# The 512 KB weight loads of the attention stage, moved from SyncE's DMA queue to GpSimd's

## The chip, the cores and the metric

One core of a Trainium2 chip runs the whole kernel. The metric is the device time of one execution in microseconds (us), lower being better.

## What is computed

The kernel is a two-layer decoder trunk for one sequence of 1024 tokens of width 1024. Layer 0 mixes tokens by causal pooling, layer 1 by attention with forget gates ("FoX", 16 heads of 64). Both also attend to 256 memory tokens, gate each branch with SiLU, project and normalise. The part that matters here is layer 1:

```
h = x @ w_in                      # queries u_main, memory queries, gates g_main, g_mem
k, v, cum = shared_kv(x, ...)     # keys, values, cumulative log forget gates
logits[t, s] = q_t . k_s / 8 + cum[t] - cum[s]     # causal, 16 heads
y_main = softmax(logits) @ v
y = concat(y_main * silu(g_main), y_mem * silu(g_mem)) @ w_out
x = layer_norm(alpha * x + y)
```

All inputs are float32 and the result must be close to float32, so each matrix operand is split into a high and a low half, and a product is made of three products of halves.

## The kernel before, in words

**Slabs.** Every projection is cut into slabs: 128 output columns for all 1024 tokens. `slab` (L324) loads the 1024 x 128 weights of one slab as two pieces of 128 x 512 float32, splits each piece into halves, and issues 48 matmuls of 128 x 512. It is a generator: it yields after each matmul, so that a caller can spread its matmuls between other work.

**Two manners of loading.** Early in the kernel each piece has its own 256 KB load on SyncE's queue (`split_w`, L212), and ScalarE and VectorE make the split. In the attention stage the flag `low[0]` is set. Then one load brings both pieces (512 KB, "wide") into a tile of pool B, which has 10 buffers; `slab` yields once, GpSimd splits the first piece, `slab` yields, GpSimd splits the second, `slab` yields, and the matmuls follow. A split on GpSimd (`gp_scaled_hi_lo`, L176 to L178) is three instructions: scale in place (L176), round to float16 (through `gp_copy`, L193), subtract (L178). The halves go into pool w, which has 6 buffers, one for a piece, so that it holds the weights of three slabs. There are 27 wide loads, numbered here from 0 in the order of their splits: gate slab 0; queries and gate of pair 1; then keys, queries and values of pairs 2 to 7, with the gates 2, 4, 7, 3, 5 and 6 between them.

**The attention stage.** `fox` walks through 16 heads and, in each, through 8 tiles of 128 queries, the longest first. A tile makes its logits on TensorE (L323), adds bias and mask and finds the bound of the exponent on VectorE (L1028), takes the exponential on ScalarE (L1036), normalises and splits into halves (L1064, L1065), transposes by DMA on SyncE's queue (L1081) and, six tiles later, multiplies with the values (L1090). The mask of a tile is made by GpSimd (`mask`, L1002), three tiles ahead, in one of the four buffers of pool raw.

**The fill.** TensorE's order is written by hand. Between the steps of a tile, `Fill.pump` issues matmuls of pending slabs, some 10 for a tile. It holds a list of units; the first is the slab at work, the second the next one. As soon as a unit is second in the list its wide load is asked for; when the slab at work has 30 of its 48 matmuls left, the next one's first piece is split, and with 16 left its second piece. The slabs of keys are asked for in other places: their load at the third tile of a pair's second head, their splits at the sixth and seventh. `ask` does the same by hand for gate slab 0, ahead of the stage.

**Queues.** TensorE's instructions stand in the written order. For the other engines a planner orders the instructions by its own simulation, ahead of the run. `tc.keep_in_program_order` pins an instruction behind the one that was written last for the same engine. The masks, the splits and the products with the gates (L1117, L1130) of GpSimd are pinned; the loads on SyncE's queue are not, so the planner may put a wide load as early as a buffer of pool B comes free. An instruction at the head of a queue that waits holds up all behind it. SyncE's queue also carries the transposes (L1081), the moves of keys and queries between partitions (L909), the forget rows (L1009) and all other loads and stores. GpSimd's queue carries 80 loads of weights early in the kernel (`look_ahead`, L258, until 260 us), and none later.

Of the kernel before, what the change touches and what calls it, by code (L numbers as in the profile page):

```python
# [78 lines left out]
def trunk_kernel(ctx, tc, x, xT, memT, win, wk, wv0, wv, wmk, wmv, wout, poolw, pscale, lng, lnb, bforget, out):  # L79
# [5 lines left out]
    nc = tc.nc  # L85
# [21 lines left out]
    def ps(shape, tag, bufs):  # L107
        return psum.tile(shape, F32, tag=tag, name=nm(tag), bufs=bufs)
# [80 lines left out]
    def three(a, b):  # L189
        return (a.hi, b.hi), (a.top, b.lo), (a.lo, b.hi if isinstance(a, Wide) else b.top)  # L190
# [18 lines left out]
    def split_w(src_dram, shape, sc=None, r=None, pin=lambda ins: ins):  # L209
        if r is None:  # L210
            r = raw(shape)
            nc.sync.dma_start(r, src_dram)  # L212
        if sc is not None:
            to = half_of(wt, shape)
            if low[0]:
                gp_scaled_hi_lo(to, r, sc)
            else:
                scaled_hi_lo(to, r, sc, pin)
            return to
        to = parts_of(wt, shape)  # L220
        (gp_hi_lo if low[0] else hi_lo)(to, r)
        return to
# [19 lines left out]
    def look_ahead(see=True):  # L242

        while to_see and len(landed) < 5:
            k, src = to_see.pop(0)
            if not room or src.shape[1] == 2:
                room[:] = [seeing[0]([P, 2 * NH])]
            r = room[0] if len(room) == 1 else room[1]
            if src.shape[1] == 2:
                r = r[:, : 2 * FW].rearrange("p (a b) -> p a b", a=2)  # L250
                room[:] = []
            elif len(room) == 1:
                room.append(r[:, NH:])
                r = r[:, :NH].rearrange("p (a b) -> p a b", a=4)
            else:
                r = r.rearrange("p (a b) -> p a b", a=4)
                room[:] = []
            tc.keep_in_program_order(nc.gpsimd.dma_start(r, src))  # L258
            landed.append((k, r))
        if landed and see:  # L260
            k, r = landed.pop(0)
            if k < 12:
                tc.keep_in_program_order(nc.vector.tensor_reduce(
                    sums[:, k : k + 1], r, AX.XY, ALU.add, apply_absolute_value=True,
                ))
            else:
                tc.keep_in_program_order(nc.scalar.activation(r, r, AF.Abs, accum_out=sums[:, k : k + 1]))
# [57 lines left out]
    def slab(pieces_dram, X, evac, banks=("pj", 2), g=0):  # L325

        arrived = isinstance(pieces_dram, list)
        sc = sws[g] if isinstance(X, Half) else None
        both = (None, None)
        if low[0]:  # L330
            wide = roomy[0]([P, 2, 4, P])
            nc.sync.dma_start(wide, pieces_dram.rearrange("c p k m -> p c k m"))
            both = wide[:, 0], wide[:, 1]
            yield 0
        ws = list(pieces_dram) if arrived else [split_w(pieces_dram[0], [P, 4, P], sc, both[0])]
        if low[0]:
            yield 0
            ws.append(split_w(pieces_dram[1], [P, 4, P], sc, both[1]))
            yield 0
        accs = {}  # L340
        high, low_top = (0,), (1, 2)
        if sc is not None:
            order = [(n, pc, (0, 1, 2)) for n in range(2) for pc in range(2)]
        elif arrived:
            order = [(n, pc, part) for pc in range(2) for n, part in ((0, high), (1, high), (1, low_top), (0, low_top))]
        else:
            order = [(0, pc, part) for part in (high, low_top) for pc in range(2)]
            order += [(1, pc, part) for part in (low_top, high) for pc in range(2)]
        seen = {0: 0, 1: 0}
        for n, pc, part in order:  # L350
            if len(ws) <= pc:
                ws.append(split_w(pieces_dram[pc], [P, 4, P], sc, both[pc]))
            if n not in accs:
                accs[n] = ps([P, NH], *banks)
            for i in part:
                a, b = three(ws[pc], X)[i]
                for k in range(4):
                    seen[n] += 1
                    nc.tensor.matmul(  # L359
                        accs[n], a[:, k, :], b[:, pc * 4 + k, n * NH : (n + 1) * NH],  # L360
                        start=seen[n] == 1, stop=seen[n] == 3 * KT,
                    )
                    if seeing[0]:
                        seeing[1] += 1
                        if seeing[1] % 8 == 0:
                            look_ahead()
                    if seen[n] == 3 * KT:
                        evac(slice(n * NH, (n + 1) * NH), accs[n])
                    yield NH
# [79 lines left out]
    def gate_units(w_dram, dst, X, g=0):  # L449
        half = hun1s[g] if isinstance(X, Half) else 0.5  # L450
        return slab(w_dram, X, lambda cols, acc: gate(acc, dst[:, cols], half), g=g)
# [9 lines left out]
    def mem_attention(l, X, kv, qtile, ytile, yd, behind=None, before=None, last=None):  # L461
# [6 lines left out]
        for h in range(MH):  # L468
            q = parts_of(qtile, [P, S])
            run(slab(win[l, 8 + h], X, lambda cols, acc: q_split(l, q[:, cols], acc)))  # L470
            qs.append(q)
            if not l:
                keys(h)
            vals(h)
# [223 lines left out]
    with tc.tile_pool(name="in0", bufs=1) as in0:  # L698
# [34 lines left out]
        def pool_group(g, see=None):  # L733
            w = WINDOWS[g]
            pms = []
            for f in (2 * g, 2 * g + 1):
                u = sb([P, S], "P", 4)
                run(slab(
                    first[f] if g == 0 else win[0, f], X, lambda cols, acc: nc.scalar.copy(u[:, cols], acc),
                    ("L", 3) if f == 1 else ("pj", 2),  # L740
                ))
                cur, sh = u, 1
                while sh < w:
                    nxt = G()
                    nc.vector.tensor_tensor(nxt[:, sh:], cur[:, sh:], cur[:, : S - sh], ALU.add)
                    nc.vector.tensor_copy(nxt[:, :sh], cur[:, :sh])
                    cur, sh = nxt, 2 * sh
                pm = G()
                nc.vector.scalar_tensor_tensor(pm[:, w - 1 :], cur[:, w - 1 :], 1.0 / w, u[:, w - 1 :], ALU.mult, ALU.subtract)
                nc.vector.tensor_tensor(pm[:, : w - 1], cur[:, : w - 1], invc[:, : w - 1], ALU.mult)  # L750
                nc.vector.tensor_tensor(pm[:, : w - 1], pm[:, : w - 1], u[:, : w - 1], ALU.subtract)
                pms.append(parts_of(T, [P, S]))
                hi_lo(pms[-1], pm)
# [543 lines left out]
```

## Time and profile before

| what | value |
|---|---|
| runs shown | 1189.03, 1192.14 and 1192.09 us; median 1192.09 us |
| the profiled execution | 1191.01 us, of which the span from first to last instruction is 1189.3 us |
| TensorE busy | 1164.2 us, 98% of the span |
| VectorE, ScalarE, GpSimd busy | 781.7, 684.7 and 285.5 us |
| granted TensorE clock | 0.995 |
| DMA | 203.89 MB, 171 GB/s on average |

The stages by time from the span's start: layer 0 until about 455 us, the memory attention of layer 1 to 577 us, first keys, values and forget gates to 645 us, the attention stage to about 1046 us, and then the output projection and the norm. In rows of instructions the columns are the start and the duration in us, the engine, the line and the operation, output<-input and count; in brackets stands how long the engine was idle just before, and who ended it. A row for a line gives minimum, median and maximum duration in ns and the first and last start. In rows of waits the columns are the total in us, how often, and the longest. PE is TensorE, DVE VectorE, ACT ScalarE, POOL GpSimd, SP SyncE; a q behind the name means its queue of instructions.

### The profile page before, as it was taken

What the parts mean: (1) busy time and instruction counts of PE and PEld (TensorE: products, weight loads), DVE (VectorE), ACT (ScalarE), POOL (GpSimd) and SP (SyncE); (2) the same over time, 40 slices, a digit from 0 to 9 for tenths busy, and PEclk for the clock granted to TensorE, in tenths of its full rate; (3) what the DMA queues carried; (4) which work ended last, traced back from release to release, by engine and by line L of the source; (5) the groups of instructions that cost most, each with busy time, mean ns of one, the idle gap of its engine ahead of it and who ended that gap; (6) DMA issues with size and microseconds to landing.
All of it is one profiled execution on the core that took longest, in us unless ns stands there. A gap on an engine that the chain in (4) does not pass through costs nothing. (4 is left out here: it accounts for less than half of the span.)

```text
span 1189.3 us, 19794 instructions
## 1 busy us (share of the span) xinstructions
PE 1164.2 (98%) x6894; PEld 672.1 (57%) x6941; DVE 781.7 (66%) x1840; ACT 684.7 (58%) x1512; POOL 285.5 (24%) x437
## 2 busy tenths in 40 slices
PE   8999999999999999999999999999999999999996
PEld 5566776555555557556674555555555545455553
DVE  6744675555765566447655888778777787874654
ACT  6478875976563234557431776666766677774210
POOL 3321001310000000000002454555554445750000
PEclk8999999999999999999999999999999999999998
DMA  7576656754286544446644789989997999875530
GB/s 259 170 250 193 171 104 213 246 179 148 89 284 170 148 136 121 133 128 124 176 148 113 172 184 220 191 171 204 187 210 150 169 195 204 217 191 171 175 109 35
DMA packets 286196, 203.89 MB, mean 171 GB/s; under 512 B 224912, under 2 KB 238352, under 8 KB 286096
## 3 DMA queue, kind: packets, MB, share of 16 engines
q1 hardware_dynamic: 279696, 181.59, 60.4%
q0 software_dynamic: 6400, 21.04, 5.4%
q8 instruction: 54, 0.88, 0.3%
q14 instruction: 46, 0.38, 0.1%
HBM read 116.01 MB, written 22.61 MB: 117 GB/s over the span
## 5 line engine op out<-in xcount | busy, mean ns | idle before, releaser
L359 PE MATMUL pj<-A,w 128*128 128x512 f16 (+2 forms) x2875 | 662.3, 383 | 4.2 <-DMA A<-A 1.2
L359 PEld LDWEIGHTS <-w 128*128 128x128 f16 (+1 forms) x2560 | 245.7, 98 | 281.2 <-issue 11.3
L1036 ACT ACTIVATE T<-MK,s 128x512 f32<-128x512 f32 x192 | 111.2, 579 | 64.6 <-DVE s L1028 47.7
L1065 DVE SCALAR_TENSOR_TENSOR P<-T,s,P 128x512 f16<-128x512 f32 x192 | 112.0, 613 | 39.1 <-ACT P L1064 38.0
L1064 ACT ACTIVATE P<-T,s 128x512 f16<-128x512 f32 x192 | 103.0, 575 | 53.1 <-issue 28.9
L599 PEld LDWEIGHTS <-T 128*128 128x128 bf16 x736 | 70.6, 98 | 89.8 <-issue 4.4
L1002 POOL TENSOR_SCALAR_AFFINE_SELECT raw<-R 128x256 f32<-128x256 f32 (+3 forms) x128 | 59.4, 466 | 178.7 <-DVE s L1028 96.2
L199 DVE TENSOR_TENSOR w<-raw,w 128x512 bf16<-128x512 f32 x74 | 52.3, 708 | 54.1 <-ACT w L198 36.7
L323 PE MATMUL L<-A 128*128 128x512 f16 (+3 forms) x384 | 84.4, 326 | 3.2 <-DVE s L1028 3.1
L885 POOL MEMSET G<- 128x128 f32 x1 | 0.2, 204 | 335.5 <-DVE V L541 335.5
L359 PEld LDWEIGHTS pj<-A,w 128*128 128x128 f32 x352 | 65.1, 188 | 16.5 <-ACT w L198 1.2
L199 DVE TENSOR_TENSOR T<-T,T 128x1024 bf16<-128x1024 f32 x23 | 28.0, 1219 | 68.8 <-PE pj L599 38.3
L178 POOL TENSOR_TENSOR w<-B,w 128x512 f16<-128x512 f32 x54 | 62.8, 1165 | 4.0
L323 PEld LDWEIGHTS <-A 128*128 128x128 f16 x384 | 37.4, 98 | 46.3 <-issue 4.8
L198 ACT CAST T<-T 128x1024 fp32r<-128x1024 f32 x23 | 24.1, 1047 | 62.6 <-DMA T<-y1d 34.9
L198 ACT CAST w<-raw 128x512 fp32r<-128x512 f32 x76 | 46.7, 615 | 23.2 <-DMA raw<-in_win_dram 9.8
L1090 PEld LDWEIGHTS <-V 128*64 128x64 f16 (+1 forms) x1152 | 50.6, 104 | 12.9 <-issue 5.6
L1090 PE MATMUL O<-T,V 128*64 128x128 f16 (+1 forms) x1152 | 57.5, 220 | 0.0
L599 PE MATMUL pj<-B,T 128*128 128x512 bf16 (+1 forms) x187 | 52.1, 385 | 0.3
L1028 DVE CUSTOM_DVE_ANT_0 MK<-L,R,scales 128x512 f32<-128x512 f32 x64 | 45.3, 708 | 9.8 <-PE L L323 9.4
L200 ACT CAST w<-raw 128x512 bf16<-128x512 f32 x78 | 48.2, 618 | 3.3 <-PE pj L359 1.9
L599 PE MATMUL L<-B,T 128*128 128x512 bf16 (+1 forms) x165 | 47.0, 394 | 0.7 <-ACT T L200 0.5
(289 smaller groups left out, 1843.5 us busy)
## 6 DMA issues: line engine op xcount, KB each, us to landing
raw<-in_win_dram SPq DMA_DIRECT2D x66, 256.0 KB, 3.3
W<-in_win_dram POOLq DMA_DIRECT2D x48, 256.0 KB, 3.8
R<-cumd SPq DMA_DIRECT2D x16, 512.0 KB, 4.4
B<-in_win_dram SPq DMA_DIRECT2D x15, 512.0 KB, 5.0
y0d<-Y SPq DMA_DIRECT2D x12, 512.0 KB, 4.0
raw<-in_wout_dram SPq DMA_DIRECT2D x24, 256.0 KB, 2.7
T<-y0d SPq DMA_DIRECT2D x12, 512.0 KB, 4.5
A<-A SPq DMA_DIRECT2D x24, 256.0 KB, 4.1
```

Source lines behind the costliest of these rows:

```text
L178: pin(nc.gpsimd.tensor_tensor(to.lo, src, to.hi, ALU.subtract))
L198: pin(nc.scalar.copy(to.hi, src))
L199: pin(nc.vector.tensor_tensor(to.lo, src, to.hi.bitcast(F32), ALU.subtract))
L200: pin((top or nc.scalar.copy)(to.top, src))
L323: nc.tensor.matmul(acc, a, b, start=i == 0, stop=i == len(terms) - 1)
L359: nc.tensor.matmul(accs[n], a[:, k, :], b[:, pc * 4 + k, n * NH : (n + 1) * NH], start=seen[n] == 1, stop=seen[n] == 3 * KT,)
L599: nc.tensor.matmul(accs[a][nh], y, w, start=kt == 8 and i == 0, stop=kt == 7 and i == 2,)
L1002: tc.keep_in_program_order(nc.gpsimd.affine_select(C[:, :w], R[:, lo:up], [[-1, w]], ALU.is_ge, -NEG, base=w - P, channel_multiplier=1,))
L1036: nc.scalar.activation(e, p[:, lo:up], AF.Exp, bias=top, scale=-1.0, accum_out=sums[:, n, hd % 2, i : i + 1],)
L1064: nc.scalar.activation(pair[:, lo:up], e, AF.Copy, scale=r)
L1065: nc.vector.scalar_tensor_tensor(pair[:, L + lo : L + up], e, r, pair[:, lo:up], ALU.mult, ALU.subtract)
L1090: nc.tensor.matmul(acc[rows, (i % 4) * P : (i % 4) * P + P], v[:, b, 2 * j : 2 * j + (1 if e else 2), :].rearrange("p e d -> p (e d)"), pt ...
```

## The change

In `slab`, the wide load goes from SyncE's queue to GpSimd's, and it is pinned there behind the GpSimd instruction that was written last. Its source, its destination, its place in the written program and everything else stay.

```diff
         if low[0]:
             wide = roomy[0]([P, 2, 4, P])
-            nc.sync.dma_start(wide, pieces_dram.rearrange("c p k m -> p c k m"))
+            tc.keep_in_program_order(nc.gpsimd.dma_start(wide, pieces_dram.rearrange("c p k m -> p c k m")))
             both = wide[:, 0], wide[:, 1]
             yield 0
```

## The prediction

> **What bounds the kernel now.** I read the page first, then the stretch in which the moved loads work, then TensorE's waits there.
>
> ```profile
> span 1189.3 us, 19794 instructions
> PE 1164.2 (98%) x6894; PEld 672.1 (57%) x6941; DVE 781.7 (66%) x1840; ACT 684.7 (58%) x1512; POOL 285.5 (24%) x437
> PEclk8999999999999999999999999999999999999998
> ```
> ```profile
> 650.00:1050.00 400.00, 395.88 (x2762) 208.67 (x2760) 316.52 (x924) 280.40 (x670) 211.21 (x318) 1.00 0.91 191
> ```
> ```profile
> PE L L323 <- DVE s L1028: 3.1, 6, 1.1
> PE pj L848 <- DVE G L857: 0.7, 1, 0.7
> PE pj L359 <- POOL w L178: 0.7, 1, 0.7
> PE pj L359 <- POOL w L193: 0.2, 1, 0.2
> ```
>
> TensorE is the bound, at full clock. From 650 to 1050 us, where 26 of the 27 wide slabs are multiplied, it is busy 395.88 of 400 us: **all its idle time there is 4.1 us**, 0.35% of the time. The waits (560 to 1060 us) say whose it is: 3.1 us belong to VectorE's softmax, 0.9 us to GpSimd's splits. The gain is capped before anything is worked out; GpSimd at 211.21 of 400 us and DMA at 0.91 are full enough to ask what can be lost.
>
> **What leaves SyncE's queue.** The line of the wide load, and the longest wait it held:
>
> ```profile
> L332 SPq DMA_DIRECT2D B<-in_win_dram x15: 367/720/1467, 517.4 to 1012.9; - x15
> L332 SPq DMA_DIRECT2D B<-in_wk_dram x6: 379/392/674, 580.5 to 792.3; - x6
> L332 SPq DMA_DIRECT2D B<-in_wv_dram x6: 421/678/1069, 581.6 to 824.8; - x6
> DMA to landing us min/median/max: 3.7/5.0/8.6
> ```
> ```profile
> SPq L332 <- POOL w L178: 26.0, 1, 26.0
> ```
>
> 27 issues leave SyncE, by medians 15 x 0.72 + 6 x 0.39 + 6 x 0.68 = 17.2 us, and a 26.0 us block near 601 us. I price both at nothing: TensorE's list of waits holds no transpose, move or forget row; six tiles between transpose and values cover them. If that cover were gone, a late transpose would show as a wait of L1090 on a DMA; there is none.
>
> **What stays in the sum: load 25.** Its row on SyncE comes after two transposes, and GpSimd and TensorE wait for it:
>
> ```profile
> 1007.68 4.38 SPq L1081 DMA_TRANSPOSE T<-P  x2
> 1012.12 1.90 SPq L332 DMA_DIRECT2D B<-in_win_dram  x2
> ```
> ```profile
> 1017.49 1.72 POOL L176 TENSOR_SCALAR B<-B,scales 128x512 f32<-128x512 f32 x2 [4.08 <-DMA B<-in_win_dram]
> ```
> ```profile
> 1018.60 1.03 PE L323 MATMUL L<-A 128*128 128x512 f16 x4
> 1019.85 1.90 PE L359 MATMUL pj<-A,w 128*128 128x512 f16 x8 [0.22 <-POOL w L193]
> 1022.45 1.47 PE L359 MATMUL pj<-A,w 128*128 128x512 f16 x6 [0.71 <-POOL w L178]
> ```
>
> Matmuls start 0.216 us apart (row of 814.72 below: 10 in 2.16 us). So after 1018.60 the next group could start at 1018.60 + 4 x 0.216 = 1019.46 and starts at 1019.85: 0.39 us. After 1019.85 the next could start eight matmuls later, at 1021.58, and starts at 1022.45: 0.87 us. Together **1.26 us**. On GpSimd the load is written where the slab before it begins, 48 matmuls (10.4 us) and some 3 us of logits and values ahead of 1019.85, so near 1006 us; issued by 1008 and 5.0 us under way it lands near 1013 instead of 1017.4. Its two splits then finish near 1018.5, ahead of TensorE. I take the whole 1.26 us off. From both sides: 0, if a buffer of pool B comes free no sooner; 4.1 us, the whole idle time, above.
>
> **What arrives on GpSimd.** The nearest rows are its early loads, half the size, and the splits:
>
> ```profile
> L258 POOL DMA_DIRECT2D W<-in_win_dram x48: 546/546/736, 24.9 to 231.5; - x48
> ```
> ```profile
> DMA to landing us min/median/max: 2.7/3.7/6.9
> ```
> ```profile
> L176 POOL TENSOR_SCALAR B<-B,scales 128x512 f32<-128x512 f32 x54 | 38.3, 709 | 4.6 <-DMA B<-in_win_dram 4.1 <-PE T L323 0.5
> L193 POOL TENSOR_SCALAR w<-B 128x512 f16<-128x512 f32 x54 | 33.7, 625 | 29.9 <-PE pj L359 25.8
> L178 POOL TENSOR_TENSOR w<-B,w 128x512 f16<-128x512 f32 x54 | 62.8, 1165 | 4.0
> ```
>
> A wide issue isn't in the trace for this queue. It describes twice the rows, so I bound it by 0.55 us (no growth) and 1.47 us (twice the slowest), and take twice the median, 1.1 us: 27 x 1.1 = 30 us more on GpSimd, 15 to 40 us by the bounds. What hides it is GpSimd's own waiting for a mask buffer:
>
> ```profile
> POOL raw L1002 <- DVE s L1028: 96.2, 48, 4.4
> POOL raw L1002 <- DVE s L1049: 53.6, 26, 4.7
> ```
>
> It waits 150 us for VectorE to give back a mask buffer, and a mask is made three tiles, some 9 us, before its use. So issues cost nothing on TensorE's path. Without that cover each would delay the logits behind it by its 1.1 us, 30 us at most.
>
> **The new wait.** Until now a wide load lay in SBUF long before its split. Load 12, the thirteenth of both lists, with TensorE's matmuls around it:
>
> ```profile
> 671.18 1.07 SPq L332 DMA_DIRECT2D B<-in_wv_dram  x1
> ```
> ```profile
> 815.83 0.69 POOL L176 TENSOR_SCALAR B<-B,scales 128x512 f32<-128x512 f32 x1
> 816.61 0.62 POOL L193 TENSOR_SCALAR w<-B 128x512 f16<-128x512 f32 x1
> 817.31 1.16 POOL L178 TENSOR_TENSOR w<-B,w 128x512 f16<-128x512 f32 x1
> 818.80 0.69 POOL L176 TENSOR_SCALAR B<-B,scales 128x512 f32<-128x512 f32 x1
> ```
> ```profile
> 812.23 2.54 PE L359 MATMUL pj<-A,w 128*128 128x512 f16 x11
> 814.72 2.32 PE L359 MATMUL pj<-A,w 128*128 128x512 f16 x10
> 816.88 1.03 PE L323 MATMUL L<-A 128*128 128x512 f16 x4
> 817.74 2.54 PE L359 MATMUL pj<-A,w 128*128 128x512 f16 x11
> 823.27 0.38 PE L359 MATMUL pj<-A,w 128*128 128x512 f16 x1
> 824.14 2.32 PE L359 MATMUL pj<-A,w 128*128 128x512 f16 x10
> 827.45 2.54 PE L359 MATMUL pj<-A,w 128*128 128x512 f16 x11
> ```
>
> It was issued 145 us ahead. Counting 48 matmuls from 812.23 (11, 10, 11, 1, 10 and 5), the slab before runs from 812.2 to 828.4, when load 12's first piece is needed. Under the change the load is issued at the start of that slab, about 812.5 to 813.6. Landing by SyncE's median of 5.0 us comes near 818, where the split was at 815.83: **GpSimd waits some 2 us per load**, with the next masks behind it, and TensorE doesn't, since the first split takes 2.64 us (815.83 to 817.31 + 1.16) and has until 828.4. The shortest slab is 48 x 0.216 = 10.4 us plus the logits of at least three tiles, 0.86 us each where long: 13 us. So TensorE is untouched while issue, landing and split fit in 13 us: 13 - 2.6 - 1.1 = **9.3 us for the landing**, against a longest of 8.6 on SyncE and 6.9 on GpSimd. Load 0 is free: its split waited for a weight buffer, not for data.
>
> ```profile
> 623.17 0.62 POOL L193 TENSOR_SCALAR w<-B 128x512 f16<-128x512 f32 x1 [25.83 <-PE pj L359]
> ```
>
> [...]
>
> **The sum.** 1191.01 (the profiled execution; the span is 1.7 us less) - 1.26 = **1189.8 us**. The median of the runs shown is 1.08 us higher than the profiled one; on its footing the sum is 1190.8. The planner will order SyncE, ScalarE and VectorE somewhat differently, which may move the 3.1 us of softmax waits either way; I count nothing for it.
>
> **The rivals.** How full SyncE's queue keeps the 16 DMA engines from 640 to 1050 us:
>
> ```profile
> q1 hardware_dynamic: 175769, 77.40, 89.2%
> ```
>
> - *Late landing; slower.* With 89.2% of their time taken by SyncE's queue, a load in a second queue may be served turn by turn among small packets. From 9.3 us of landing on, TensorE waits; each further us costs 1 us at each of the 19 slabs that the fill asks for (27 less six of keys, gate 0 and gate 7, whose loads are asked three tiles ahead). At 11 us that is 1.7 x 19 = 32 us: 1223. Against it: 8.6 us was the worst on SyncE, behind the transposes of its own queue. Chance 0.09.
> - *Thin places; slower.* GpSimd's 2 us waits delay splits and masks, and where it also stands behind a product with a gate (L1117, which waits for VectorE), nothing is left. With 2 us lost at 3 of the 27 slabs: 1191.0 + 6 - 1.3 = 1195.8 us, up to 1199 with five. The wait on a DMA at L176 in the row of 1017.49 shows that the kind exists. Chance 0.20.
> - *Load 25 no sooner; no change.* Its buffer, not SyncE's queue, held it: 1191.0. Chance 0.12.
> - *The softmax waits go too; faster.* The emptier SyncE queue or new order removes all 4.1 us: 1186.9. Chance 0.06.
>
> **How the numbers follow.** Forecast 0.53; a measurement of this kernel can tell about 0.3%, 3.6 us, from no change. Within it lie the forecast and the third rival, 0.65; faster by more, the fourth, 0.06; slower by more, the first two, 0.29. The range goes from 1186.9, the whole idle time, to 1199, the upper end of thin places, and leaves out the late landing.
>
> **What would show it.** Right: L332 as POOL rows of about 1.1 us, landing in 4 to 8 us; L176 waiting on DMA about 2 us in some 19 places; L359's waits on GpSimd gone near 1020 us; busy TensorE near 396 of 400 us. Wrong: L359 waiting on L178 or L193 in many slabs, or L323 on VectorE behind late masks (L1002).

## The result, and the profile after

Over eight runs of each on one chip the changed kernel takes 1196.9 us (median; 1193.63 to 1202.63) and the kernel before 1191.4 us (1189.03 to 1192.14). The ratio is **1.0061, 95% interval 1.0048 to 1.0074**: slower by 0.6%. The profiled execution took 1196.06 us, 5.05 us more than that of before. The page, and then the stretch from 650 to 1050 us (busy time and count of PE, weight loads, VectorE, ScalarE and GpSimd, granted clock, DMA share, GB/s):

```profile
span 1194.3 us, 19817 instructions
PE 1169.4 (98%) x6941; PEld 675.2 (57%) x6941; DVE 784.4 (66%) x1840; ACT 685.6 (57%) x1512; POOL 303.7 (25%) x464
```
```profile
650.00:1050.00 400.00, 390.31 (x2724) 207.02 (x2723) 311.02 (x904) 275.67 (x657) 223.22 (x337) 0.99 0.96 198
```

TensorE's idle time there went from 4.1 to 9.7 us, and the mean clock is no longer full. Its list of waits (560 to 1060 us) names the new releaser at once; both GpSimd rows of before are gone:

```profile
PE O L1090 <- DMA T<-P: 5.8, 3, 2.9
PE L L323 <- DVE s L1028: 3.8, 5, 1.2
```

L1090 on a DMA is a product with the values that waits for its transposed tile. The prediction had named this row as the sign of a lost cover, and had taken its absence before the change as proof that the cover was there. Neither of the signs that it gave for being wrong (many waits of L359 on a split, late masks) appeared.

**Where on the time line.** Products with the values stand in the same order in both kernels, so the start of each can be compared. The starts of some of them, by TensorE's time lines:

| group | before | after | after minus before |
|---|---|---|---|
| first of the stage | 672.97 | 669.76 | -3.21 |
| second to tenth | 684.37 to 785.45 | 681.17 to 782.27 | -3.17 to -3.27 |
| eleventh | 798.27 | 797.74 | -0.53 |
| twelfth and 13th | 810.08, 820.96 | 810.93, 821.81 | +0.85 |
| 14th to 22nd | 833.60 to 936.20 | 834.02 to 936.63 | +0.42 or +0.43 |
| 23rd and 24th | 947.29, 959.11 | 948.14, 959.95 | +0.85, +0.84 |
| 25th and 26th | 970.41, 983.72 | 970.84, 984.15 | +0.43 |
| 27th | 995.68 | 999.10 | +3.42 |
| 28th | 1010.08 | 1014.90 | +4.82 |
| 29th | 1025.04 | 1028.58 | +3.54 |
| 30th | 1039.44 | 1044.39 | +4.95 |
| 31st | 1050.60 | 1055.56 | +4.96 |

Over 21 of the 30 steps from a group to the next nothing changes by more than 0.1 us. The stage loses 4.96 + 3.21 = 8.2 us, almost all of it in **two places**, 4.0 us near 797 and 4.4 us near 999 (+0.43 to +4.82). The 3.2 us by which this execution enters the stage early aren't credited to the change: they come from small waits ahead of 645 us, and a variant below whose loads are those of before until the last ones enters nearly as early (670.4). In all traces but one (gp_free's, below) the stage begins between 668.4 and 673.0 us, so one execution of each kernel can't tell whether the change has a part in the early start. If it has none, the 8.2 us of this stage are more than the 5.5 us between the medians, and that difference stays open.

TensorE's rows at the two places (the bracket is idle time and its releaser), behind a like group of before:

```profile
820.96 2.48 PE L1090 MATMUL O<-T,V 128*64 128x128 f16 x52
```
```profile
794.78 0.38 PE L359 MATMUL pj<-A,w 128*128 128x512 f16 x1
797.74 3.86 PE L1090 MATMUL O<-T,V 128*64 128x128 f16 x52 [2.57 <-DMA T<-P]
...
999.10 3.87 PE L1090 MATMUL O<-T,V 128*64 128x128 f16 x52 [2.92 <-DMA T<-P]
```
```profile
795.00:797.00 2.00, 0.16 (x1) 0.00 (x0) 1.35 (x4) 0.07 (x1) 0.00 (x0) 1.00 1.23 187
797.00:799.00 2.00, 1.26 (x24) 1.27 (x26) 1.19 (x5) 1.38 (x3) 1.62 (x3) 0.59 1.25 261
799.00:801.00 2.00, 2.00 (x27) 1.83 (x22) 0.51 (x1) 0.70 (x2) 1.33 (x2) 0.56 0.38 71
801.00:803.00 2.00, 2.00 (x20) 1.27 (x18) 0.91 (x3) 1.33 (x3) 0.00 (x0) 1.00 1.00 190
```

Each place costs twice: the wait, and then the same 52 matmuls at a lower granted clock, 3.86 and 3.87 us instead of 2.48. The stretches above are those of the first place, with 0.59 and 0.56; at the second the clock was 0.50 and then 0.71 from 999 to 1003 us. 2.57 + 1.38 = 3.95 us and 2.92 + 1.39 = 4.31 us are the two steps of the table. The clock was 0.50 from 797.4 to 800.7 us, beginning within the idle time of 2.57 us, and from 998.8 to 1002.1 us, beginning within that of 2.92 us; from 801 to 803 and from 1003 to 1005 us it was 1.00. The like group of before ran at 1.00.

**Why the transposes are late near 797.** GpSimd's two issues ahead of it, and SyncE's queue from its time line (start, duration from first to last of the group, line):

```profile
764.90 0.76 POOL L332 DMA_DIRECT2D B<-in_win_dram  x1
766.24 0.74 POOL L332 DMA_DIRECT2D B<-in_wk_dram  x1
```
```profile
764.86 2.85 SPq L1081 DMA_TRANSPOSE T<-P  x1
767.80 10.95 SPq L909 DMA_DIRECT2D A<-A  x3
778.87 4.10 SPq L1081 DMA_TRANSPOSE T<-P  x2
790.78 7.84 SPq L1081 DMA_TRANSPOSE T<-P  x3
```
```profile
771.31 4.84 SPq L909 DMA_DIRECT2D A<-A  x3
```
```profile
DMA to landing us min/median/max: 8.7/10.3/11.8
```

The row of 771.31 is before's counterpart of the three moves, and the last one the landing of the two loads. In the changed kernel the loads of a gate and of keys go out 1.3 us apart and take 8.7 and 11.8 us to land; the transpose issued beside them takes 12.2 us, the first two moves 10.5 and 9.1 us. The third move waits for the moves ahead of it and stands at the head of SyncE's queue for 8.2 us (before, the longest wait of a move for other moves was 4.0 us from 650 to 1050 us), so the three moves take 10.95 us instead of 4.84 and everything behind them is late. The product waits for the first of the three transposes in the row of 790.78: it lands at 797.7, and the product starts at 797.74. Before the change its counterpart landed at 794.29, 4.0 us ahead of its product.

The DMA traffic shows the sharing itself. Each row gives a queue's packets, its MB and the share of the 16 DMA engines' time that they took: first the changed kernel from 768 to 777 us (q0 carries GpSimd's loads, q1 all of SyncE's transfers), then the kernel before from 771 to 780 us.

```profile
q0 software_dynamic: 286, 1.05, 55.2%
q1 hardware_dynamic: 932, 0.46, 43.4%
```
```profile
q1 hardware_dynamic: 2481, 1.48, 88.2%
```

Nearly the same bytes moved in both, but beside the loads SyncE's transfers got about half of the engines' time that they had before.

At 999 only one wide load is near (issued 992.12); SyncE's transposes were some 4 us late already, which I could not put down to one cause. The place is not peculiar to the changed kernel: half_bytes and keys_late, below, still wait 1.7 and 1.5 us near 995 us.

Landing times (minimum, median, maximum) of transposes, before and after, show it over the whole run:

```profile
DMA to landing us min/median/max: 2.8/4.8/7.3
```
```profile
DMA to landing us min/median/max: 2.7/5.1/12.2
```

### The profile page after: what moved, and what is told of

It is laid out like the page before. It is cut to its first block, busy times and chain, and to the rows that moved or that the text cites. A ratio compares the mean times of both kernels' runs of the same rounds, so it can differ in the third digit from the quotient of the medians.

```text
span 1194.3 us, 19817 instructions
## 1 busy us (share of the span) xinstructions
PE 1169.4 (98%) x6941; PEld 675.2 (57%) x6941; DVE 784.4 (66%) x1840; ACT 685.6 (57%) x1512; POOL 303.7 (25%) x464
## 5 line engine op out<-in xcount | busy, mean ns | idle before, releaser
L359 PE MATMUL pj<-A,w 128*128 128x512 f16 (+2 forms) x2896 | 663.6, 383 | 1.2 <-ACT MK L200 0.6
L359 PEld LDWEIGHTS <-w 128*128 128x128 f16 (+1 forms) x2560 | 246.0, 98 | 278.2 <-issue 9.7
L359 PEld LDWEIGHTS pj<-A,w 128*128 128x128 f32 x352 | 65.1, 188 | 17.1 <-ACT w L198 1.7
L1090 PE MATMUL O<-T,V 128*64 128x128 f16 (+1 forms) x1152 | 60.3, 227 | 5.8 <-DMA T<-P 5.8
L1090 PEld LDWEIGHTS <-V 128*64 128x64 f16 (+1 forms) x1152 | 53.2, 108 | 19.1 <-issue 8.5
L176 POOL TENSOR_SCALAR B<-B,scales 128x512 f32<-128x512 f32 x54 | 37.5, 696 | 52.5 <-DMA B<-in_win_dram 22.4
```

The lines of the kernel that those rows point to most:

```text
L359: nc.tensor.matmul(accs[n], a[:, k, :], b[:, pc * 4 + k, n * NH : (n + 1) * NH], start=seen[n] == 1, stop=seen[n] == 3 * KT,)
L1090: nc.tensor.matmul(acc[rows, (i % 4) * P : (i % 4) * P + P], v[:, b, 2 * j : 2 * j + (1 if e else 2), :].rearrange("p e d -> p (e d)"), pt ...
```

## The experiments

**Theory A:** loads in a queue of their own are served beside the transposes instead of behind them, so transposes and moves land later, and TensorE waits at the values. **Theory B:** the loads are merely asked for too late by the written place, and whatever queue they stand in makes no difference. **Theory C**, which some of the expectations name: GpSimd stands at L176 until a load has landed, and what it does next is late. None of them concerns GpSimd's 0.76 us for an issue.

The planner orders each kernel anew. By the traces, ScalarE and VectorE keep one and the same order in all kernels but act_pinned. Of SyncE's 480 transfers other than wide loads, 472 keep their order from before to after and 479 from before to gp_free; after, half_bytes, keys_early and two_halves have one order. Each trace is of one execution, which can lie some us off its kernel's median (half_bytes 1193.9 for 1190.4, keys_late 1191.4 for 1193.6).

For each kernel I counted, from its trace, the mean landing time of the L1081 transposes by the number of wide loads in flight with them (in brackets how many transposes; in the last column, spare_loads has two or more, keys_early one more with three). A slow transpose meets more loads, so the columns overstate the effect. Counted instead by the loads in flight when a transpose is issued, the contrast stays: beside one load 5.31 us before and 6.54 us after.

| kernel | none | one | two |
|---|---|---|---|
| before (same queue) | 4.63 (59) | 5.20 (35) | 5.50 (2) |
| sp_pinned (same queue) | 4.44 | 4.97 | 5.12 |
| after | 4.60 (38) | 5.77 (56) | 10.73 (2) |
| gp_free | 4.53 | 6.06 | 6.58 |
| act_pinned | 4.77 | 5.54 | 8.43 |
| half_bytes | 4.64 | 5.44 | 6.93 |
| keys_early | 4.68 | 5.94 (52) | 7.29 (8) |
| keys_late | 4.40 | 5.94 (66) | - |
| spare_loads | 4.69 | 5.87 | 7.30 (40) |

**sp_pinned**: the written place, on SyncE's own queue.

```diff
-            tc.keep_in_program_order(nc.gpsimd.dma_start(wide, ...))
+            tc.keep_in_program_order(nc.sync.dma_start(wide, ...))
```

> The wide load in the written place, but on SyncE's queue. Theory A (sharing): what costs is a load in a queue of its own, which the DMA engines serve in turn with SyncE's transposes and moves; on SyncE's queue the late place costs little: 1189 to 1193 us, transposes landing in under 5.0 us at the median, no wait of L1090 on a DMA. Theory B (late asking): what costs is that the loads come a slab ahead instead of ten, whatever the queue: 1195 to 1199 us. Theory C (GpSimd held): GpSimd's waits for landings at L176 cost; they stay here, so 1195 to 1199 us too.

Measured 1229.7 against 1190.45 us, ratio 1.0325 (1.0309 to 1.0342), far above what any of the three theories expected. TensorE's waits, and GpSimd's at the first step of a split:

```profile
PE pj L359 <- POOL w L193: 26.8, 7, 7.6
```
```profile
  POOL B L176: 61.8, 14
```
```profile
768.22 0.60 SPq L332 DMA_DIRECT2D B<-in_wv_dram  x1
```

The transposes stay quick (5.0 us beside one load), and the loads land in 5.0 us, but they are issued late: a pinned load stands behind whatever SyncE is held up by. Load 8, the row shown, landed at 773.7 for a slab that starts at about 776. So lateness is expensive on SyncE, and of another kind: TensorE waits for splits (L193), which it never does in the changed kernel. The two parts of the change, queue and place, don't simply add.

**gp_free**: GpSimd's queue, but not pinned, so that the planner issues loads as early as before.

```diff
-            tc.keep_in_program_order(nc.gpsimd.dma_start(wide, ...))
+            nc.gpsimd.dma_start(wide, ...)
```

> The wide load on GpSimd's queue, but not pinned, so that the planner puts it as early as a buffer is free. A: the sharing stays, wherever the loads fall beside transposes: 1194 to 1198 us. B: 1189 to 1193 us, as before. C: GpSimd no longer waits at L176, 1189 to 1193 us.

Measured 1200.8 us, ratio 1.0085 (1.007 to 1.01). TensorE's waits, GpSimd's, and one of TensorE's rows:

```profile
PE T L323 <- DMA T<-P: 6.1, 1, 6.1
PE O L1090 <- DMA T<-P: 5.4, 2, 4.4
```
```profile
  POOL B L176: 5.0, 2
```
```profile
704.00 4.06 PE L1090 MATMUL O<-T,V 128*64 128x128 f16 x52 [4.40 <-DMA T<-P]
```

GpSimd almost never waits for a load, so nothing is late, and the orders of SyncE, ScalarE and VectorE are those of before but for one transfer. The kernel is still slower, and TensorE's new waits are for transposes: neither B nor C can explain this. Loads 2, 3 and 4, issued together at 573.5 to 575.0 us, landed after 4.7, 11.0 and 12.0 us, and the first wait shown, from 587.7 to 593.7, is for a transpose of the memory attention (L509), issued at 580.86, that took 12.8 us beside loads; the second follows load 13, issued at 693.15 and landed after 10.6 us.

**half_bytes**: places and queue of the change; the second piece of weights isn't loaded, and the first is used twice, so this kernel leaves out half of each slab's weights. (A second line of the edit, not shown, lets the second split scale by 1, since the first has scaled the piece in place.)

```diff
-            tc.keep_in_program_order(nc.gpsimd.dma_start(wide, ...))
-            both = wide[:, 0], wide[:, 1]
+            tc.keep_in_program_order(nc.gpsimd.dma_start(wide[:, 0], pieces_dram[0]))
+            both = wide[:, 0], wide[:, 0]
```

> The changed kernel in which each wide load brings only the first of its two pieces, which both splits then use (the second piece of the weights is left out of the result). Same issues, same places, half the bytes. A: half as long in flight beside the transposes, 1190 to 1193 us. B: the loss hangs on asking late, a landing about 1 to 1.5 us sooner gives back under half: 1194 to 1196 us. C: the same as B, 1193 to 1196 us, as GpSimd's waits shrink with the landing.

Measured 1190.4 us, ratio 1.0003 (0.9991 to 1.0014): the loss is gone, which B and C didn't expect.

```profile
PE O L1090 <- DMA T<-P: 1.7, 1, 1.7
PE pj L359 <- POOL w L193: 0.6, 1, 0.6
```
```profile
  POOL B L176: 29.5, 11
```

GpSimd still issues 27 loads at the same places and still waits for them at L176, in 11 places; TensorE waits for a split once, 0.6 us. SyncE, ScalarE and VectorE have the order of the changed kernel. What went is the weight of the loads beside the transposes: 5.44 us instead of 5.77 beside one, 6.93 instead of 10.73 beside two (two transposes each). GpSimd's issue is also 0.17 us shorter, and its waits at L176 are 29.5 us instead of 46.6.

**keys_early** and **keys_late**: the load of the keys is asked for at another tile, to part it from the gate's load.

```diff
-                    if b and pr < 7 and i in (2, 5, 6):
-                        if i == 2:
+                    if b and pr < 7 and i in (0, 5, 6):      # keys_early
+                        if i == 0:
+                    if b and pr < 7 and i in (4, 6, 7):      # keys_late
+                        if i == 4:
```

> The changed kernel with the loads of the keys' slabs asked for two tiles earlier (first instead of third tile of the pair's second head), so that no two wide loads are issued within 4 us. A: the wait near 797 us goes, since two loads in flight together caused it, and half of the loss with it: 1192 to 1195 us; transposes beside two wide loads none. B and C: the loads are as late as before for all other slabs, 1196 to 1198 us.

> The changed kernel with the loads of the keys' slabs asked for two tiles later (fifth tile, splits at the seventh and eighth), so that the loads of a gate and of keys in pairs 2 and 4 no longer go out 1 to 3 us apart. A, in its narrow form (two loads in flight together make the loss): 1191 to 1194 us. A, in its wide form (each load beside transposes delays them, and the thinnest place waits): 1195 to 1198 us, with waits of L1090 elsewhere.

keys_early: 1197.0 us, ratio 1.0051 (1.003 to 1.0072). Its trace still has both loads 1.1 us apart (770.4 and 871.4 us), so it didn't part them there. It shows something else: nearly the whole loss is back, with 0.4 us of waits at L1090. Its longest wait, and the row of ScalarE that stands behind it:

```profile
PE L L323 <- DVE s L1049: 2.7, 1, 2.7
```
```profile
735.72 0.69 ACT L1064 ACTIVATE P<-T,s 128x512 f16<-128x512 f32 x1 [1.86 <-DMA T<-P]
```

A transpose issued at 722.93 took 12.7 us beside a single load, issued at 723.37, that took 12.0. ScalarE waits 1.86 us for it, VectorE 1.75 us for ScalarE, and TensorE's logits near 738.8 for VectorE. So late transposes also reach TensorE by way of the softmax, and one load is enough.

keys_late: 1193.6 us, ratio 1.0025 (1.0014 to 1.0037); no two loads are within 8 us of each other.

```profile
PE O L1090 <- DMA T<-P: 1.5, 1, 1.5
```

Of the three waits at L1090 one of 1.5 us is left, and more than half of the loss is given back. Keeping loads apart helps, then, but by keys_early pairs are not the whole cause: a single load can make a transpose as late.

**act_pinned**: the same, on ScalarE's queue.

```diff
-            tc.keep_in_program_order(nc.gpsimd.dma_start(wide, ...))
+            tc.keep_in_program_order(nc.scalar.dma_start(wide, ...))
```

> The wide loads in the written place, on ScalarE's queue instead of GpSimd's. Theory A (sharing): any queue but SyncE's shares the DMA engines with SyncE's transposes, 1194 to 1200 us, transposes beside one wide load at 5.6 us or more at the median. Rival D (GpSimd's kind of load): the harm is that of loads described by GpSimd; on ScalarE's queue transposes beside a load stay near 5.0 us and the time is 1189 to 1193 us. Either way ScalarE gains 27 issues, which may cost TensorE 0 to 3 us.

Measured 1196.9 us, ratio 1.0042 (1.0026 to 1.0058). Its issues cost half as much as GpSimd's, and its landings are quick (median 5.3 us):

```profile
L332 ACTq DMA_DIRECT2D B<-in_win_dram x15: 374/375/434, 637.1 to 1032.0; - x15
```
```profile
PE L L323 <- issue: 4.2, 1, 4.2
```

The loss isn't peculiar to GpSimd's way of loading. But only 1.1 us of TensorE's waits are at L1090; the longest, 4.2 us at the logits, has no releaser that the profile shows. It ends at 995.93, 0.09 us after a move (L909) issued at 993.45 has landed, so the move is its likely end; why that move is late stays open, since no wide load was in flight beside it. VectorE's order differs much here (1226 of 1840 instructions keep it), so how far this loss is the same one stays open too.

**late_only**: the kernel before, with loads 25 and 26 alone on GpSimd, to have the predicted gain by itself.

```diff
+            tc.keep_in_program_order(nc.gpsimd.dma_start(wide, ...)) if late[0] else nc.sync.dma_start(wide, ...)
...
-            yield next(units)
+            late[0] = pr > 3; n = next(units); late[0] = False; yield n
```

> The kernel before with only loads 25 and 26 on GpSimd's queue. The prediction's step (load 25 lands some 4 us sooner, 1.26 us off TensorE's path): 1189 us against 1190.4, waits of L359 on GpSimd near 1020 us gone. Against it: those two loads share with transposes too and the gain is lost: 1190.5 to 1192 us.

Measured 1192.2 us, ratio 1.0012 (1.0001 to 1.0023): no gain, as the expectation's second case had it (1190.5 to 1192 us). TensorE's rows at slab 25 and a little later:

```profile
1016.93 3.19 PE L359 MATMUL pj<-A,w 128*128 128x512 f16 x14
...
1029.71 0.38 PE L323 MATMUL L<-A 128*128 128x256 f16 x2 [1.54 <-DVE s L1028]
```

Slab 25 runs without a wait; its load was issued at 1007.55 and landed at 1013.00. Some 13 us later logits wait 1.54 us for VectorE's softmax.

**spare_loads**: the kernel before, which also loads each wide slab but the first a second time, on GpSimd's queue, into two tiles that nobody reads (pool B has eight buffers instead of ten).

```diff
             nc.sync.dma_start(wide, ...)
+            tc.keep_in_program_order(nc.gpsimd.dma_start(spare[len(asked) % 2], ...))
```

> The kernel before with its own loads in place on SyncE, and in addition a load of the same weights on GpSimd's queue in the changed kernel's places, into two spare buffers that nothing reads (pool B has 8 buffers left for the rest). Nothing waits for these loads. A: beside them the transposes are late and TensorE waits for them: 1196 to 1205 us, L1090 waiting on DMA. B (late asking) and C (GpSimd held at its splits): nothing is asked late and no split waits: 1190 to 1193 us.

Measured 1212.0 us, ratio 1.0168 (1.0127 to 1.0209).

```profile
PE O L1090 <- DMA T<-P: 6.7, 5, 2.6
PE L L323 <- issue: 6.1, 1, 6.1
PE pj L359 <- POOL w L193: 3.6, 1, 3.6
```

With twice the bytes five products with values wait, for transposes that take 7.30 us beside two or more loads. No instruction reads the added data, so at L1090 the traffic is the likely cost. The smaller pool is a second suspect, but its wide loads stand no longer at the head of SyncE's queue: 16.9 us from 650 to 1050 us, against 17.3 before. The wait of 6.1 us ends at 694.66, 0.09 us after a move (L909) has landed that took 5.6 us beside an added load, so it is likely of the same kind. The wait for a split (L193) shows that this is not all.

**two_halves** and **two_halves_keys_late**: the wide load goes out as two loads of 256 KB, one for each split, alone and with the edit of keys_late.

```diff
-            tc.keep_in_program_order(nc.gpsimd.dma_start(wide, ...))
+            tc.keep_in_program_order(nc.gpsimd.dma_start(wide[:, 0], pieces_dram[0]))
             both = wide[:, 0], wide[:, 1]
-            yield 0
+            yield 0; tc.keep_in_program_order(nc.gpsimd.dma_start(wide[:, 1], pieces_dram[1]))
```

> The changed kernel with each wide load made as two loads of 256 KB on GpSimd's queue, the second asked for where the first piece is split, so the same bytes in bursts of half the size. Theory A in its narrow form (the size of the burst makes single transposes and moves late): loss of about a third to a half of the changed kernel's, 1192 to 1195 us. A in its wide form (the bytes in all that share with the transposes): 1195 to 1199 us, as with whole loads.

> Both: halves, and the keys' loads asked for two tiles later, so that no two loads go out within 4 us. Narrow form: 1190 to 1192 us, no loss left against before. Wide form: 1193 to 1197 us. Neither expects it to be faster than the kernel before by more than 1 us, since TensorE's other waits are VectorE's.

Measured 1194.2 and 1195.5 us against 1191.7, ratios 1.0032 (1.0013 to 1.0051) and 1.004 (1.0019 to 1.0061). Of each, TensorE's waits:

```profile
PE pj L359 <- POOL w L193: 2.9, 1, 2.9
PE L L323 <- ACT P L1064: 2.8, 1, 2.8
PE O L1090 <- DMA T<-P: 0.7, 1, 0.7
```
```profile
PE pj L359 <- POOL w L193: 3.6, 4, 2.2
PE O L1090 <- DMA T<-P: 0.3, 1, 0.3
```

The waits at L1090 nearly go, and others take their place: the second half is asked for later, and its split is late (L193). I did not follow the wait of 2.8 us at the logits. Both together are no better than one. No version is faster than the kernel before.

## Why the prediction was wrong

The sum said 1189.8 us; the median is 1196.9, 5.5 us above the kernel before: slower by more than 3.6 us, to which the prediction gave 0.29. It lies inside the range only because the range reached up to a rival that did not happen, so that is luck. By its steps:

- **"What leaves SyncE's queue ... I price both at nothing: ... six tiles between transpose and values cover them." This step failed.** It took the absence of a wait for a large margin. Counted from the trace of before, the last transpose for a product of the four longer tiles lands typically 2.5 to 4.3 us ahead of it, in the closest case 0.04 us (695.05 for 695.10); for the four shorter tiles it is 3.7 to 12.9 us. Six tiles lie between *logits* and values, and the softmax and SyncE's queue have used up most of them by the time the transpose lands. While the loads stood in SyncE's own queue, transposes beside one were little slower (5.20 us before, 4.97 in sp_pinned). In the changed kernel one transpose took 12.2 us and the moves held SyncE for 8.2 us; the eleventh product, which had 4.0 us of margin before, waited 2.57 us. The step priced the issues that left, and not what the transposes then share the DMA engines with.
- **What two queues do to each other**, which the sum left out, was the point. The prediction had it in the rival "late landing" alone, and there for the load; it hit the transposes. The runs show the sharing: in the 9 us from 768 GpSimd's and SyncE's queue took 55.2% and 43.4% of the engines' time, and in each 2 us from 768 to 776 us both moved packets (63 and 55, 97 and 430, 49 and 293, 43 and 126). Beside one load a transpose takes 5.20 us when both are in SyncE's queue and 5.77 us when the load is in another, and 5.50 against 10.73 beside two, though the two-load figures of these two kernels rest on two transposes each. How the engines choose between the queues is not shown.
- **Load 25, -1.26 us: right, and worth nothing.** From the 28th to the 29th group of the table the loss falls by 1.28 us, and slab 25's row has no wait:

```profile
1024.28 3.19 PE L359 MATMUL pj<-A,w 128*128 128x512 f16 x14
```

  By the 30th group 1.41 us are lost again, to the softmax, as in late_only. The load itself was issued later than the step assumed, at 1014.40, and landed at 1019.8; in late_only it went out and landed as assumed (1007.55 and 1013.0). The step didn't ask what is late next.
- **GpSimd's issue, 1.1 us: the size was off, the cover right.** It took 0.76 us at the median, within the bounds of 0.55 and 1.47, and 0.78 us at the longest. GpSimd's row of the load, and two of its waits from 640 to 1050 us:

```profile
L332 POOL DMA_DIRECT2D B<-in_win_dram x15: 751/763/780, 594.3 to 1030.6; - x15
```
```profile
POOL raw L1002 <- DVE s L1028: 63.8, 37, 3.8
POOL raw L1002 <- DVE s L1049: 38.1, 19, 5.6
```

  The waits for mask buffers shrank from 149.8 to 101.9 us and took in issues and new waits; no late mask delays the logits.
- **The new wait at L176: right in kind, larger in size.** Predicted some 2 us in 19 places, measured 46.6 us in 15, 3.1 us each, since landing takes 4.2 to 11.8 us (median 6.5) and not 5.0. TensorE waits for no split in the stage, so the rival "thin places", whose price of 1195.8 to 1199 us comes nearest to the median, named the wrong place: the thin place is SyncE's queue. That its price fits is chance.
- **Not in the sum at all:** the clock after a wait. In this execution it made 1.38 + 1.39 us of the 8.2.

What is shown: TensorE's new waits are for transposes. Loads in a queue of their own are enough for a loss, in the order of before and with no load late (gp_free). The issues on GpSimd and the waits at L176 cost nothing that can be measured, since half_bytes keeps 27 issues, of 0.59 us, and 29.5 us of the waits. Half the bytes take the whole loss away, in the order of the changed kernel, and loads kept apart take more than half. Left open are the late start near 999, the early start of the stage, act_pinned's late move, and why the two remedies that leave the work whole don't add.

## What to carry to other kernels

That an engine's list of waits has no row for a transfer says nothing of the margin: measure from landing to first use, and take the smallest. Here a large load in the same queue made an urgent transfer less late (5.20 us against 4.63 without one) than a load in another queue did (5.77 against 4.60). Before moving loads out, ask what they will run beside, and keep them apart from each other and from the transfers that are waited for. A gain at one wait counts once the next latest input is known, here the softmax right behind slab 25.

## What the runs showed of the hardware

- A 512 KB load did not land sooner in a queue of its own than in the full one: median 6.5 us on GpSimd's queue (5.4 in gp_free) and 5.3 on ScalarE's, against 5.0 on SyncE's; longest 11.8 us on GpSimd's against 8.6.
- GpSimd's issue took 0.59 us at the median for half of a wide load (half_bytes) and 0.76 us for a whole one, and ScalarE's 0.375 us for a whole one (act_pinned). The row of half_bytes:

```profile
L332 POOL DMA_DIRECT2D B<-in_win_dram x15: 553/590/602, 595.1 to 1027.6; - x15
```

- At the end of an idle time of 2.57 us the granted clock was 0.59 and 0.56 in two stretches of 2 us (797 to 801 us), and at the end of one of 2.92 us 0.50 and 0.71 (999 to 1003 us). With one of 2.2 us it was 0.50 in sp_pinned (841 to 843 us) and 1.00 in two_halves_keys_late (1021 to 1027 us).
